# Delta rule: keys, queries, values and turned keys in two fixed sets of tiles, and four steps that load less

## The chip, the cores and the metric

The kernel runs on one core of a Trainium2 chip. The metric is the device time of one execution, in microseconds (us). Beside timed runs there is one profiled execution, with the time of every instruction and transfer.

## The reference, cut to what matters

The program is a two-layer backbone over 256 context tokens and 512 latent tokens of width 1024. Layer 0 mixes with a bidirectional gated delta rule, layer 1 with attention. The change touches only the delta rule of layer 0, which for one direction and one chunk of 64 tokens does this with its state `s`, a 128 x 128 matrix per head:

```python
def step(s, xs):
    qk_i, qd_i, kd_i, u_i, w_i, gl_i = xs
    v_new = u_i - jnp.einsum('bhcd,bhde->bhce', w_i, s)
    o = jnp.einsum('bhcd,bhde->bhce', qd_i, s) + jnp.einsum('bhcs,bhse->bhce', qk_i, v_new)
    s = s * gl_i[..., None, None] + jnp.einsum('bhcd,bhce->bhde', kd_i, v_new)
    return s, o

def bidir_delta(q, k, v, g, beta, s0_f, s0_b):
    o_f, s_f = chunk_gated_delta(q, k, v, g[:, 0], beta[:, 0], s0_f)
    ...
    o_b, s_b = chunk_gated_delta(fl(q), fl(k), fl(v), fl(g[:, 1]), fl(beta[:, 1]), s0_b)
    return o_f + fl(o_b), s_f, s_b
```

There are 16 value heads and 8 key heads. First the 4 context chunks are run from a zero state, both ways, then the 8 latent chunks from the two states that this leaves.

## The kernel before, in words

**Pairs of chunks.** The two directions run at the same time. A step takes one chunk of the forward direction and one of the backward direction, 64 + 64 = 128 partitions. Chunk p and chunk n - 1 - p make up pair t; there are 2 pairs of context and 4 of latent tokens. Each pair is met twice (`visit` 0 and 1), the second time with the directions exchanged, so there are 12 steps `s` = 0 to 11, which work on the pairs 0, 1, 1, 0, then 2, 3, 4, 5, 5, 4, 3, 2.

**What a step needs from DRAM.** The keys k (`k_d`), the queries q (`q_d`), the values v (`v_d`, as two halves of 64 partitions), the turned keys kt (`kt_d`), all four the same at both visits of a pair; and the inverse T (`t_d`) and the decayed product Q K (`qk_d`), which differ by visit. Each of k, q, each half of v, T, Q K and kt is a transfer of 512 KB. Each step but step 0 loads all of it. Step 0 needs no k and q, because its state is zero; its T, Q K, kt and v are loaded ahead by `first_matrices` and `first_values` (L1026 to L1034).

**Where it lies.** Odd steps take tiles of the pool `ch`, made at L1526. Even steps take tiles of the pool `even`: four buffers of the tag `df` (`even_tile`, L1018) for T, Q K, kt and k, and the tag `C` (`values_tile`, L1015) for v. The queries take two buffers of the tag `kq1` in turn. The pool `ch` stands where the pool of the stage before stood, so its first loads can begin only when that stage has let go of the memory.

**The work of a step.** A step is four parts of four heads (`x` = 4 s + p). `products(x)` (L1567) multiplies the state by k and by q (L1585; one matrix product group with k, one with q, for each of two key heads), subtracts from v on VectorE (L1588), scales the query product on ScalarE (L1591) and decays the state on GpSimd (L1594). `solve(x)` (L1600) applies T (L1611). `update(x)` (L1629) applies Q K (L1640) and kt (L1648). They are written in the order products(x), solve(x-1), update(x-2).

**What sets the order.** On TensorE, VectorE, ScalarE and GpSimd the order is as written (`manual_schedule`, L1771). The SyncE queue (SP), which issues the loads, is not held to it: a planner places its loads as soon as their tile is free by its reckoning, among loads that are free at once in the order of the program. Each engine and queue then runs strictly in the order so found. The load helpers are

```python
    def matrices_loaded(t, visit, Tt, QK, kt):
        dma(Tt, t_d[t, :, visit])
        dma(QK, qk_d[t, :, visit])
        return dma(kt, kt_d[t]).ins
```

and `values_loaded` (L1009), which issues the two halves of v. `mark` holds a step's last load; the first loads of the next stage's weights and gates (L1812) are queued behind it at steps 7, 8, 9 and 10.

Of the kernel before, what the change touches and what calls it, by code (L numbers as in the profile page):

```python
# [8 lines left out]
F32 = mybir.dt.float32  # L9
# [8 lines left out]
P = 128  # L18
# [5 lines left out]
QH, VH = 8, 16  # L24
# [45 lines left out]
def pair_info(t):  # L70
    if t < 2:
        return t, 4, 0
    return t - 2, 8, NCTX
# [13 lines left out]
def backbone(tc, a, out):  # L87
    nc = tc.nc
    V, S, G, T = nc.vector, nc.scalar, nc.gpsimd, nc.tensor
    dma = nc.sync.dma_start  # L90
# [8 lines left out]
    def dtile(shape, name):  # L99
        return dram.tile(shape, F32, tag=name, name=name)  # L100
# [6 lines left out]
    k_d = dtile([NT, P, QH, P], "k_d")  # L107
    q_d = dtile([NT, P, QH, P], "q_d")
    kt_d = dtile([NT, P, QH, P], "kt_d")
# [4 lines left out]
    t_d = dtile([NT, P, 2, VH, 64], "t_d")  # L114
    qk_d = dtile([NT, P, 2, VH, 64], "qk_d")
# [70 lines left out]
    def rsqrt_steps(x, mul, out=None, room=None):  # L186

        n = x.shape[1]
        rcount[0] += 1
        y, t = (rsp.tile([P, NT * VH], F32, tag=f"rs{i}", name=f"rs{i}_{rcount[0]}")[:, 0:n] for i in range(2))  # L190
        if room is not None:
            t = room
        yi = y.bitcast(I32)
        steps = [
            lambda: V.tensor_scalar(x, x, mul, EPS, ALU.mult, ALU.add),
            lambda: V.tensor_scalar(yi, x.bitcast(I32), -0.5, float(0x5F3759DF), ALU.mult, ALU.add),
        ]
        for i in range(3):
            to = (x if out is None else out) if i == 2 else y
            steps += [  # L200
                lambda: V.scalar_tensor_tensor(t, x, -0.5, y, ALU.mult, ALU.mult),
                lambda: V.tensor_tensor(t, t, y, ALU.mult),
                lambda to=to: V.scalar_tensor_tensor(to, t, 1.5, y, ALU.add, ALU.mult),
            ]
        return steps
# [797 lines left out]
# [6 lines that stand above are left out]
    def values_loaded(t, v, h0=0, h1=VH):  # L1009
        p, n, base = pair_info(t)  # L1010
        for hf, c in ((0, p), (1, n - 1 - p)):
            c += base // 64
            dma(v[hf * 64:hf * 64 + 64, h0:h1], v_d[c // 2, c % 2 * 64:c % 2 * 64 + 64, h0:h1])

    def values_tile(s):  # L1015
        return room["even"].tile([P, 2, 32, 32], F32, tag="C", name=f"cv_{s}").rearrange("p a b c -> p (a b c)").rearrange("p (h d) -> p h d", d=P)

    def even_tile(s, nm):  # L1018
        return room["even"].tile([P, VH, 64], F32, tag="df", name=f"c{nm}_{s}", bufs=4)

    def by_key_heads(x):
        return x.rearrange("p h c -> p (h c)").rearrange("p (h d) -> p h d", d=P)

    opening = {}

    def first_matrices():  # L1026
        T_, QK, kt = (even_tile(0, nm) for nm in ("T", "QK", "kt"))
        opening["m"] = T_, QK, by_key_heads(kt)
        matrices_loaded(0, 0, *opening["m"])
# [112 lines left out]
    last = {}  # L1142
    T0 = 134

    def kept(name, piece):
        last[name] = piece
        return piece
# [29 lines left out]
    ck = Piece("DVE", 0.4, 0.0, biases_kept, after=[pv], holds=[("tr", pv)], lands=0.1, slack=0.1)  # L1177
# [17 lines left out]
    for q in range(4):  # L1195
# [7 lines left out]
        for k in (2 * q, 2 * q + 1):  # L1203
            y_ = None
            for i in range(2):
                f = at + 2.5 * (k % 2) + 0.6 * i
# [43 lines left out]
    for h in range(QH):  # L1250
# [4 lines left out]
        else:  # L1255
            wh, wl = k_weights(h, t0)
            g, owners = [], []
            for i in range(2):
                n = 1 if h == 1 else 4
# [28 lines left out]
    c = []  # L1288
# [48 lines left out]
    for n, (c, h) in enumerate(heads):  # L1337
        t0 = T0 + n * SLOT
        w = kept(("w", n), Piece("SP", 0.4, t0 - 30, w_load, n, takes=["w"], sent=1.3, since=-99.0))
# [38 lines left out]
    def keys_and_rows(t, queries, due, since=0.0, after=()):  # L1378
        k = Piece("SP", 1.0 + queries, due, keys_loaded, t, queries, takes=["kq", "kq"], sent=1.3 + 1.3 * queries, since=since, after=list(after) + row_loads[-2:-1], behind=late_pieces)
        for v in range(2):  # L1380
            row_loads.append(Piece("SP", 2.0 - queries, due, decay_rows, t, v, not queries, takes=["df"], sent=2.4, since=since, after=row_loads[-1:] or [k]))
        return k, row_loads[-2:]
# [18 lines left out]
    for t, due in enumerate(T0 + x for x in (-14, -15, 45, 126, 140, 160)):  # L1401
        k, r = keys_and_rows(t, False, due - 12, since=max(T0 + 24.0, due - 14))
# [39 lines left out]
    for t, due in enumerate(T0 + x for x in (275, 280, 320, 685, 710, 820)):  # L1442
        k, r = keys_and_rows(t, True, due - 12, after=[last["stored", "q", h] for h in range(QH)])
# [4 lines left out]
        for v in range(2):  # L1448
            G_ = (t, v) not in ((0, 0), (0, 1), (1, 0), (1, 1), (2, 0), (2, 1), (3, 0), (3, 1), (4, 0), (4, 1), (5, 0), (5, 1))
            pr = Piece("POOL" if G_ else "DVE", 2.42 if G_ else 1.22, due + 8, q_prod, t, v, G if G_ else V, port=1, after=[ma, d_[v]], holds=[("df", r[v]), (f"KQ{v}", ma)], lands=0.1)  # L1450
            qprev.append(pr)
            kept(("QK", t, v), Piece("SP", 1.3, due + 14, q_store, t, v, after=[pr], holds=[("df", r[v])], sent=2.2))
    Piece("DVE", 2.4, T0 + N * SLOT - 5, lambda: [f_() for f_ in rsqrt_steps(rq.rearrange("p t h -> p (t h)"), 1.0)], after=[last["rq", h] for h in range(QH)], since=T0 + 376.0)

    at = T0 + N * SLOT - 60
    Piece("SP", 1.2, at, first_matrices, after=[last["T", 0], last["QK", 0, 0], last["QK", 5, 0], last["QK", 5, 1]], takes=["df", "df", "df"], sent=5.0)
    fv = []
# [12 lines left out]
    ch = ch_c.__enter__()  # L1470
# [52 lines left out]
    if True:  # L1523
        ch.tile([P, 4, P], F32, tag="r0", name="r_0", bufs=1)
        St = [ch.tile([P, 2, 2, P], F32, tag=f"S{hh}", name=f"S{hh}", bufs=1) for hh in range(QH)]
        for tag, shape, n in (("vn", [P, 4, P], 2), ("vd", [P, 4, P], 2), ("T", [P, VH, 64], 1), ("v", [P, VH, P], 1), ("QK", [P, VH, 64], 1),  # L1526
                              ("kt", [P, QH, P], 1), ("kq0", [P, QH, P], 1), ("kq1", [P, QH, P], 2), ("o", [P, 4, P], 2), ("r1", [P, 4, P], 1)):
            for i in range(n):
                ch.tile(shape, F32, tag=tag, name=f"{tag}_first{i}", bufs=n)

        def where(s):
            n, sl, base = (4, s, 0) if s < 4 else (8, s - 4, 2)
            visit = 0 if sl < n // 2 else 1
            return base + (sl if visit == 0 else n - 1 - sl), visit

        loads = {}
        mark = [None]

        def load_step(s):
            nm = f"_{s}"  # L1540
            t, visit = where(s)
            if s == 0:
                (Tt, QK, kt), v = opening["m"], opening["v"]
                loads[s] = (None, kt, v, Tt, QK)
                return
            if s % 2:
                Tt = ch.tile([P, VH, 64], F32, tag="T", name="cT" + nm, bufs=1)
                v = ch.tile([P, VH, P], F32, tag="v", name="cv" + nm, bufs=1)
                QK = ch.tile([P, VH, 64], F32, tag="QK", name="cQK" + nm, bufs=1)
                kt = ch.tile([P, QH, P], F32, tag="kt", name="ckt" + nm, bufs=1)  # L1550
            k0 = ch.tile([P, QH, P], F32, tag="kq0", name="ck" + nm, bufs=1) if s % 2 else by_key_heads(even_tile(s, "k"))
            if not s % 2:
                Tt, QK = even_tile(s, "T"), even_tile(s, "QK")
                kt, v = by_key_heads(even_tile(s, "kt")), values_tile(s)
            kq = [k0, ch.tile([P, QH, P], F32, tag="kq1", name="cq" + nm)]
            for w, src in enumerate((k_d, q_d)):
                dma(kq[w], src[t])
            values_loaded(t, v)
            mark[0] = matrices_loaded(t, visit, Tt, QK, kt)
            loads[s] = (kq, kt, v, Tt, QK)  # L1560

        live = {}
        prq = [pcx.tile([P, 2, 4, P], F32, tag=tag, name=f"{tag}_all", bufs=1) for tag in ("pr", "pq")]
# [1 line left out]
        def products(x):  # L1567

            s, p = divmod(x, 4)
            if p == 0:  # L1570
                load_step(s)
# [362 lines left out]
    for n in range(32):  # L1934
# [5 lines left out]
        if n in (16, 19, 21, 24):  # L1940
            k0 = {16: 0, 19: 2, 21: 4, 24: 6}[n]
# [35 lines left out]
        if n in (18, 20, 23, 25):  # L1977
            k0 = {18: 0, 20: 2, 23: 4, 25: 6}[n]
# [217 lines left out]
    def q_cosines(p, t):  # L2196
        x = q_bank(p, t).rearrange("p (h d) -> p h d", h=2)
        o = tmp.tile([P, 2, P], F32, tag="qr", name=f"qr{p}{t}", bufs=2)
        V.tensor_tensor(o, x, bcast(cg[0][:, t], 1, 2), ALU.mult)
        return o  # L2200
# [179 lines left out]
    for u in range(32 + 4):  # L2380
        piece = pieces1[u] if u < len(pieces1) else None
        last = (q_products, 0, 3) if u == 0 else pieces1[u - 1] if u <= len(pieces1) else None
# [6 lines left out]
        o = None  # L2389
        if last and last[0] is q_products:  # L2390
            q_squares(*last[1:])
            o = q_cosines(*last[1:])
# [20 lines left out]
        for half in range(2):  # L2413
            if piece and piece[0] is q_products:
                q_products(*piece[1:], range(half * 4, half * 4 + 4))
            elif piece:
                k0 = 4 * (u % 2) + 2 * half
# [29 lines left out]
        if u == 23:  # L2447
# [4 lines left out]
            for k in range(KT):  # L2452
                w = wp.tile([P, D], F32, tag="w", name=f"wf{k}", bufs=3)
# [149 lines left out]
```

## Time and profile before

| | |
|---|---|
| median of 3 runs | 1144.64 us (1141.11 to 1145.9) |
| time of the profiled execution | 1139.69 us |
| its span | 1137.5 us |
| TensorE busy (matmul) | 1106.4 us, 97% |
| VectorE, ScalarE, GpSimd busy | 787.5, 746.9, 603.1 us |
| bytes moved | 208.69 MB |
| the twelve steps | from about 535.4 to 712 us of the span |

PE is TensorE's matmul, PEld its weight load, DVE is VectorE, ACT is ScalarE, POOL is GpSimd, SPq and ACTq are the queues from which SyncE and ScalarE issue transfers. In a timeline a row has the start, the duration, the engine, the line, the operation, output <- inputs, the number of instructions and in brackets the idle time before it with what ended it. In a table of transfers the last number is the time from issue to landing. Names lose their numbers: `cq` is the queries of any step, `ck` the keys, `cv` the values, `cT`, `cQK` and `ckt` the three matrices. `q1` is the transfer queue of SP, `q10` that of ACT, `q8` fetches TensorE's instructions.

### The profile page before, as it was taken

What the parts mean: (1) busy time and instruction counts of PE and PEld (TensorE: products, weight loads), DVE (VectorE), ACT (ScalarE), POOL (GpSimd) and SP (SyncE); (2) the same over time, 40 slices, a digit from 0 to 9 for tenths busy, and PEclk for the clock granted to TensorE, in tenths of its full rate; (3) what the DMA queues carried; (4) which work ended last, traced back from release to release, by engine and by line L of the source; (5) the groups of instructions that cost most, each with busy time, mean ns of one, the idle gap of its engine ahead of it and who ended that gap; (6) DMA issues with size and microseconds to landing.
All of it is one profiled execution on the core that took longest, in us unless ns stands there. A gap on an engine that the chain in (4) does not pass through costs nothing. (4 is left out here: it accounts for less than half of the span.)

```text
span 1137.5 us, 27228 instructions
## 1 busy us (share of the span) xinstructions
PE 1106.4 (97%) x10511; PEld 903.7 (79%) x10511; DVE 787.5 (69%) x1628; ACT 746.9 (66%) x1990; POOL 603.1 (53%) x525
## 2 busy tenths in 40 slices
PE   5999999999999999999999999999999999999997
PEld 2677788888888888888666666788877889989886
DVE  4785666688889988774678788445555477667647
ACT  4453554477787888756689888875776356666731
POOL 0564111329999999960675598656744353130820
PEclk9999999999999999999999999999999999999999
DMA  9489753765738887665998994676854112101323
GB/s 366 180 305 324 253 159 118 228 174 171 219 129 245 280 233 222 182 229 164 280 279 249 276 257 116 207 213 183 247 148 139 37 58 73 38 19 57 111 75 93
DMA packets 117106, 208.69 MB, mean 183 GB/s; under 512 B 12113, under 2 KB 76786, under 8 KB 111730
## 3 DMA queue, kind: packets, MB, share of 16 engines
q1 hardware_dynamic: 97202, 195.71, 55.8%
q10 hardware_dynamic: 19776, 11.25, 3.3%
q8 instruction: 83, 1.36, 0.5%
q14 instruction: 45, 0.37, 0.1%
HBM read 166.16 MB, written 40.67 MB: 182 GB/s over the span
## 5 line engine op out<-in xcount | busy, mean ns | idle before, releaser
L1768 PE MATMUL po<-woh,y 128*128 128x512 f32 x384 | 129.3, 401 | 0.0
L1706 POOL TENSOR_TENSOR wol<-wo,woh 128x1024 fp32r<-128x1024 f32 x32 | 77.3, 2416 | 54.3 <-ACT woh L1699 51.1
L810 POOL TENSOR_TENSOR X<-X,tmp 128x62 f32<-128x62 f32 (+15 forms) x93 | 99.5, 1070 | 7.3
L1594 POOL TENSOR_TENSOR S<-S,glb 128x512 f32<-128x512 f32 x80 | 81.8, 1044 | 36.4 <-PE ks L1585 36.1
L809 POOL TENSOR_TENSOR tmp<-L,X 128x62 f32<-128x62 f32 (+15 forms) x93 | 91.0, 979 | 6.7
L929 PE MATMUL g_z<-uh,wh_z 128*128 128x512 f32 (+1 forms) x256 | 88.0, 344 | 0.0
L929 PE MATMUL g_v<-uh,wh_v 128*128 128x512 f32 (+1 forms) x256 | 87.9, 344 | 0.0
L944 DVE SCALAR_TENSOR_TENSOR acc_v<-g_v,cwv,acc_v 128x510 f32<-128x510 f32 (+3 forms) x128 | 77.7, 614 | 14.7 <-ACT acc_v L936 11.3
L929 PE MATMUL g_z<-ul,wh_z 128*128 128x512 f32 (+1 forms) x256 | 86.2, 337 | 0.5 <-issue 0.5
L929 PE MATMUL g_v<-ul,wh_v 128*128 128x512 f32 (+1 forms) x256 | 86.1, 336 | 0.0
L929 PE MATMUL g_v<-uh,wl_v 128*128 128x512 f32 (+1 forms) x256 | 86.1, 336 | 0.0
L929 PE MATMUL g_z<-uh,wl_z 128*128 128x512 f32 (+1 forms) x256 | 86.1, 336 | 0.0
L1768 PEld LDWEIGHTS po<-woh,y 128*128 128x128 f32 x384 | 72.3, 188 | 15.5 <-issue 0.3
L1768 PE MATMUL po<-wol,y 128*128 128x512 f32 x192 | 75.5, 393 | 0.0
L1734 DVE SCALAR_TENSOR_TENSOR pt<-pt,og,z 128x128 f32<-128x128 f32 x96 | 34.4, 358 | 33.3 <-PE pt L1725 31.0
L555 POOL TENSOR_TENSOR kt<-kt,kss 128x768 f32<-128x768 f32 x8 | 11.6, 1472 | 85.6 <-DVE kss L183 57.0
L1585 PE MATMUL ks<-S,ck 128*64 128x256 f32 x352 | 55.5, 392 | 0.9 <-ACT o L1591 0.9
L1662 DVE TENSOR_TENSOR S<-su,S 128x512 f32<-128x512 f32 x80 | 51.5, 686 | 5.1 <-PE su L1648 3.4
L1588 DVE SCALAR_TENSOR_TENSOR r<-ks,negV,cv 128x128 f32<-128x128 f32 x176 | 52.4, 344 | 3.6 <-DMA cv<-v_d 1.9
L1585 PE MATMUL ks<-S,cq 128*64 128x256 f32 x352 | 53.7, 379 | 0.0
L929 PEld LDWEIGHTS g_z<-ul,wh_z 128*128 128x128 f32 x256 | 48.6, 190 | 5.4 <-issue 0.7
L929 PEld LDWEIGHTS g_z<-uh,wh_z 128*128 128x128 f32 x256 | 48.5, 190 | 5.2
(469 smaller groups left out, 3341.5 us busy)
## 6 DMA issues: line engine op xcount, KB each, us to landing
aw<-in_ada_late SPq DMA_DIRECT2D x16, 1024.0 KB, 7.5
wo<-in_dn_w_out SPq DMA_DIRECT2D x32, 512.0 KB, 3.9
cv<-v_d SPq DMA_DIRECT2D x22, 512.0 KB, 9.6
aw<-in_ada_first SPq DMA_DIRECT2D x8, 1024.0 KB, 11.4
w_z<-in_dn_w_in SPq DMA_DIRECT2D x16, 512.0 KB, 6.2
w_v<-in_dn_w_in SPq DMA_DIRECT2D x16, 512.0 KB, 4.8
v_d<-vt ACTq DMA_DIRECT2D x16, 384.0 KB, 4.2
cT<-t_d SPq DMA_DIRECT2D x12, 512.0 KB, 9.1
```

The costliest lines, as they stand in the source:

```text
L555: G.tensor_tensor(kt, kt, bcast(r[:, h % 2 * NT:(h % 2 + 1) * NT], 2, P), ALU.mult)
L809: G.tensor_tensor(tv, bcast(L[:, :, j + 1:, j], 3, j + 1), bcast(X[:, :, j, 0:j + 1], 2, n), ALU.mult)
L810: G.tensor_tensor(X[:, :, j + 1:, 0:j + 1], X[:, :, j + 1:, 0:j + 1], tv, ALU.subtract)
L929: T.matmul(ps[:, :m], w[:, k], u[:, k, c0:c0 + m], start=k == 0 and n_ == 0, stop=k == KT - 1 and n_ == 2)
L944: V.scalar_tensor_tensor(acc[:, c0 + lo:c0 + hi], ps[:, lo + j - 2:hi + j - 2], cwv[:, j, ct:ct + 1], acc[:, c0 + lo:c0 + hi], ALU.mult, A ...
L1585: T.matmul(ks[r0:r0 + 64, w], kq[w][:, hh, r0:r0 + 64], St[hh][:, d], start=True, stop=True)
L1588: V.scalar_tensor_tensor(r[:, 2 * j + i], ks[:, 0, i], negV[:, visit, t, h:h + 1], v[:, h], ALU.mult, ALU.add)
L1594: G.tensor_tensor(St[hh], St[hh], bcast(g_, 3, P), ALU.mult)
L1662: V.tensor_tensor(St[hh], sj, St[hh], ALU.add)
L1706: G.tensor_tensor(wl, raws.pop(n), halves[n][0], ALU.subtract)
L1734: V.scalar_tensor_tensor(pj, pj, og, raw(z, off, [[st_, 2], [1, 64]]), ALU.mult, ALU.mult)
L1768: T.matmul(acc[nh], y[i][:, j, :], ww[k][:, nh * 512:(nh + 1) * 512], start=h == 0 and x == 0, stop=h == VH - 1 and x == 2)
```

## The change

The tiles for T, v, Q K, kt, k and q of the pool `ch` are made once, in the same sizes and the same order as before, and named: `qB` and `qA` stand where the two buffers of `kq1` stood. There are two sets of k, q, v, kt. Set A is the even pool's k, v and kt with `qA`; set B is the odd pool's k, v and kt with `qB`. Steps take the sets in the order A B B A B A B A A B A B. T and Q K go by even and odd step as before.

Steps 2, 8 and 9 work on the pair of the step before or of three steps before, whose set is still on the chip: they load only T and Q K. Step 3 finds v and kt of step 0 in set A and loads T, Q K, k and q. At step 1 the load of q is issued after T and Q K and ahead of kt; in the other steps that load it, it stays behind k. All else is as it was.

```diff
+        work = [(("vn", [P, 4, P], 2), ("vd", [P, 4, P], 2)), (("o", [P, 4, P], 2), ("r1", [P, 4, P], 1))]
+        odd = {}
...
+        for nm, shape in (("T", [P, VH, 64]), ("v", [P, VH, P]), ("QK", [P, VH, 64]), ("kt", [P, QH, P]), ("k", [P, QH, P]), ("qB", [P, QH, P]), ("qA", [P, QH, P])):
+            odd[nm] = ch.tile(shape, F32, tag=nm, name="c" + nm, bufs=1)
...
+        (T0, QK0, kt0), v0 = opening["m"], opening["v"]
+        homes = {"A": (by_key_heads(even_tile(0, "k")), odd["qA"], v0, kt0), "B": (odd["k"], odd["qB"], odd["v"], odd["kt"])}
+
         def load_step(s):
-            nm = f"_{s}"
             t, visit = where(s)
+            k, q, v, kt = homes["ABBABABAABAB"[s]]
+            Tt, QK = (odd["T"], odd["QK"]) if s % 2 else (T0, QK0)
+            loads[s] = ((k, q), kt, v, Tt, QK)
             if s == 0:
...
-            kq = [k0, ch.tile([P, QH, P], F32, tag="kq1", name="cq" + nm)]
-            for w, src in enumerate((k_d, q_d)):
-                dma(kq[w], src[t])
-            values_loaded(t, v)
-            mark[0] = matrices_loaded(t, visit, Tt, QK, kt)
-            loads[s] = (kq, kt, v, Tt, QK)
+            fresh = s not in (2, 8, 9)
+            if fresh:
+                dma(k, k_d[t])
+                if s > 1:
+                    dma(q, q_d[t])
+                if s != 3:
+                    values_loaded(t, v)
+            dma(Tt, t_d[t, :, visit])
+            last = dma(QK, qk_d[t, :, visit])
+            if s == 1:
+                dma(q, q_d[t])
+            if fresh and s != 3:
+                last = dma(kt, kt_d[t])
+            mark[0] = last.ins
```

More of the change, by code (lines that the diff above doesn't have):

```diff
@@ L1525, in backbone @@
         St = [ch.tile([P, 2, 2, P], F32, tag=f"S{hh}", name=f"S{hh}", bufs=1) for hh in range(QH)]
-        for tag, shape, n in (("vn", [P, 4, P], 2), ("vd", [P, 4, P], 2), ("T", [P, VH, 64], 1), ("v", [P, VH, P], 1), ("QK", [P, VH, 64], 1),
-                              ("kt", [P, QH, P], 1), ("kq0", [P, QH, P], 1), ("kq1", [P, QH, P], 2), ("o", [P, 4, P], 2), ("r1", [P, 4, P], 1)):
+        work = [(("vn", [P, 4, P], 2), ("vd", [P, 4, P], 2)), (("o", [P, 4, P], 2), ("r1", [P, 4, P], 1))]
+        odd = {}
+        for tag, shape, n in work[0]:
+            for i in range(n):
+                ch.tile(shape, F32, tag=tag, name=f"{tag}_first{i}", bufs=n)
+        for nm, shape in (("T", [P, VH, 64]), ("v", [P, VH, P]), ("QK", [P, VH, 64]), ("kt", [P, QH, P]), ("k", [P, QH, P]), ("qB", [P, QH, P]), ("qA", [P, QH, P])):
+            odd[nm] = ch.tile(shape, F32, tag=nm, name="c" + nm, bufs=1)
+        for tag, shape, n in work[1]:
             for i in range(n):
@@ L1537, in backbone @@
         mark = [None]
+        (T0, QK0, kt0), v0 = opening["m"], opening["v"]
+        homes = {"A": (by_key_heads(even_tile(0, "k")), odd["qA"], v0, kt0), "B": (odd["k"], odd["qB"], odd["v"], odd["kt"])}
         def load_step(s):
-            nm = f"_{s}"
             t, visit = where(s)
+            k, q, v, kt = homes["ABBABABAABAB"[s]]
+            Tt, QK = (odd["T"], odd["QK"]) if s % 2 else (T0, QK0)
+            loads[s] = ((k, q), kt, v, Tt, QK)
             if s == 0:
-                (Tt, QK, kt), v = opening["m"], opening["v"]
-                loads[s] = (None, kt, v, Tt, QK)
                 return
[L1546 to L1554, printed above, removed]
-            kq = [k0, ch.tile([P, QH, P], F32, tag="kq1", name="cq" + nm)]
-            for w, src in enumerate((k_d, q_d)):
-                dma(kq[w], src[t])
-            values_loaded(t, v)
-            mark[0] = matrices_loaded(t, visit, Tt, QK, kt)
-            loads[s] = (kq, kt, v, Tt, QK)
+            fresh = s not in (2, 8, 9)
[12 more added lines that the diff above has]
+            mark[0] = last.ins
         live = {}
```

## The prediction

> **What bounds the kernel now.** I read the page first, for the share of each engine.
>
> ```profile
> span 1137.5 us, 27228 instructions
> PE 1106.4 (97%) x10511; PEld 903.7 (79%) x10511; DVE 787.5 (69%) x1628; ACT 746.9 (66%) x1990; POOL 603.1 (53%) x525
> ```
>
> TensorE is busy nearly throughout, but that is an average. So I cut the delta rule's stretch into its steps, each from its first product to the next step's (stretch, then the busy time of PE, PEld, DVE, ACT, POOL, the granted clock, the DMA share and GB/s).
>
> ```profile
> 535.38:542.20 6.82, 4.93 (x114) 3.35 (x113) 4.01 (x13) 3.46 (x7) 1.19 (x2) 1.00 1.04 201
> 542.20:557.30 15.10, 15.10 (x260) 9.78 (x257) 10.97 (x26) 10.35 (x30) 9.33 (x10) 1.00 0.86 273
> 557.30:574.96 17.66, 15.59 (x261) 10.10 (x257) 12.15 (x29) 13.04 (x41) 13.17 (x12) 1.00 1.02 297
> 574.96:590.06 15.10, 15.10 (x258) 9.79 (x257) 12.39 (x29) 11.31 (x36) 12.39 (x12) 1.00 1.01 276
> 680.66:695.76 15.10, 15.10 (x260) 9.78 (x256) 12.43 (x29) 14.37 (x53) 14.10 (x17) 1.00 0.81 234
> ```
>
> A step takes 15.10 us, all of it PE, and it takes as long where the transfer engines are 81% busy as where they are 101% busy. So the loads cost nothing as such; they cost only where a product waits for one. Step 2 (557.30 to 574.96) alone is longer, by 17.66 - 15.10 = 2.56 us. That is the most that taking loads away can give in these steps. The timeline of PE and DVE shows where it sits:
>
> ```profile
> 560.10 1.04 PE L1648 MATMUL su<-vd,ckt 64*64 64x256 f32 x16
> 560.67 1.13 DVE L1588 SCALAR_TENSOR_TENSOR r<-ks,negV,cv 128x128 f32<-128x128 f32 x4 [1.85 <-DMA cv<-v_d]
> 562.06 0.65 PE L1585 MATMUL ks<-S,ck 128*64 128x256 f32 x4 [0.91 <-ACT o L1591]
> ...
> 569.61 0.65 PE L1585 MATMUL ks<-S,ck 128*64 128x256 f32 x4
> 571.97 0.60 PE L1640 MATMUL pq_all<-vn,cQK 64*64 64x128 f32 x13
> 573.73 0.32 PE L1640 MATMUL pq_all<-vn,cQK 64*64 64x128 f32 x2 [1.16 <-issue]
> 574.96 0.65 PE L1585 MATMUL ks<-S,ck 128*64 128x256 f32 x4
> ```
>
> A quarter of a step is 15.10 / 4 = 3.775 us. The second quarter of step 2 begins at 562.06 instead of 557.30 + 3.775 = 561.08: 0.98 us late, because DVE waited 1.85 us for v, then ACT for DVE, then PE for the buffer that ACT empties. The fourth quarter lasts 574.96 - 569.61 = 5.35 us, 1.58 us too long, with PE standing between two like matmuls for no reason that the profile shows ("issue"). The two make 2.56.
>
> **The opening, where one load moves.** Next I read the queue of SP at step 1, and the landing times of the transfers issued between 530 and 549 us.
>
> ```profile
> 490.52 0.98 SPq L1557 DMA_DIRECT2D ck<-k_d  x1
> 530.50 0.83 SPq L1557 DMA_DIRECT2D ck<-k_d  x1
> 531.38 0.42 SPq L1557 DMA_DIRECT2D cq<-q_d  x1
> 531.85 1.10 SPq L1013 DMA_DIRECT2D cv<-v_d  x2
> 533.04 0.53 SPq L1005 DMA_DIRECT2D cT<-t_d  x1
> 533.61 0.45 SPq L1006 DMA_DIRECT2D cQK<-qk_d  x1
> 536.25 0.34 ACTq L852 DMA_DIRECT2D t_d<-Tt  x1
> 548.35 0.32 SPq L1007 DMA_DIRECT2D ckt<-kt_d  x1
> 549.35 0.32 SPq L1557 DMA_DIRECT2D cq<-q_d  x1
> ```
>
> ```profile
> cv<-v_d SPq DMA_DIRECT2D x2, 512.0 KB, 8.4
> t_d<-Tt ACTq DMA_DIRECT2D x1, 1024.0 KB, 12.1
> ck<-k_d SPq DMA_DIRECT2D x1, 512.0 KB, 4.1
> cq<-q_d SPq DMA_DIRECT2D x1, 512.0 KB, 6.6
> cT<-t_d SPq DMA_DIRECT2D x1, 512.0 KB, 12.8
> cQK<-qk_d SPq DMA_DIRECT2D x1, 512.0 KB, 14.9
> ckt<-kt_d SPq DMA_DIRECT2D x1, 512.0 KB, 3.9
> ```
>
> Start plus landing time: k at 534.6, q at 538.0, v at about 540.3, T at 545.8, Q K at 548.5. The six loads, 3 MB, land in the order of issue, the last 18.0 us after the first issue, while a 1 MB store of ACT shares the same engines until 536.25 + 12.1 = 548.35. And this is when PE wants them:
>
> ```profile
> 542.20 0.65 PE L1585 MATMUL ks<-S,ck 128*64 128x256 f32 x4
> 542.68 0.60 PE L1585 MATMUL ks<-S,cq 128*64 128x256 f32 x4
> 547.85 0.67 PE L1611 MATMUL pr_all<-r,cT 64*64 64x128 f32 x16
> 552.11 0.62 PE L1640 MATMUL pr_all<-vn,cQK 64*64 64x128 f32 x16
> 552.55 1.04 PE L1648 MATMUL su<-vd,ckt 64*64 64x256 f32 x16
> ```
>
> q is wanted at 542.68, T at 547.85, Q K at 552.11, kt at 552.55. Today each is there: q with 4.7 us to spare, T with 2.0, Q K with 3.6, kt (548.35 + 3.9 = 552.25) with 0.3.
>
> **The change part by part.** *Loads removed.* Steps 2, 8 and 9 lose five each (k, q, two halves of v, kt), step 3 loses three: 18 transfers of 512 KB, 9 MB of the 208.69. At steps 3, 8 and 9 nothing waits for them, so this gives 0: PE's own 15.10 us are the cover. At step 2 the late v is no longer loaded, so the 0.98 us go. For the 1.58 us there are bounds: 0 if it has nothing to do with traffic, 1.58 if the fetch of PE's instructions stood behind the loads. Between 571 and 574 us the transfer engines show
>
> ```profile
> q1 hardware_dynamic: 234, 0.88, 95.0%
> q8 instruction: 1, 0.02, 2.9%
> ```
>
> and PE's own waits between 520 and 730 us hold this "issue" wait and no second one:
>
> ```profile
> PE pq_all L1640 <- issue: 1.2, 1, 1.2
> ```
>
> A fetch of instructions fell in just this stretch, among loads that took 95% of the engines. I take 1.58, since in the changed kernel steps 2 and 3 load 3 MB in place of 7. [...]
>
> *Fixed tiles.* Same sizes in the same order, so `qB` lies where step 1's q lay. Each load waits for the last reader of the same place, two steps back, as before: 0. The k that went out at 490.52 for step 2 was for the even pool's tile, which is now A's k and is filled for step 3: 0. If it is not sent early, see the second rival.
>
> *q of step 1 moved behind two halves of v, T and Q K.* On SP the four others move up by q's 0.47 us (531.85 - 531.38). Q K then goes out at 533.14 and takes its 0.45, so q goes out at about 533.6 in place of 531.38. The work of the engines is the same, 3 MB issued before ACT's store; only the order is new. By order of issue Q K takes T's place (545.8) and q takes Q K's place: 548.5. PE asks at 542.68. PE takes its work in order, so behind that product stand the second head pair, the last `solve` of step 0 and its last two updates; ACT, POOL and DVE wait for these, and so do T and Q K of step 2, whose tiles they free. Cost: 548.5 - 542.68 = 5.8 us. From below: a transfer that runs alone took 3.9 (kt), which would bring q at 537.5 and cost 0. From above: q could be held to the end of both of ACT's stores, after the second of which SP issued at 549.35: 6.7. I take 5.8, for q's neighbours in that queue took 12.8 and 14.9 us, not 3.9.
>
> [...]
>
> *What the delay covers.* Everything behind shifts by 5.8 us. kt of step 1 still goes out at 548.35 and now has 6.1 us to spare. T and Q K of step 2 shift with the products that free them and with those that use them, and have k, q, v and kt of step 2 no longer around them. q of step 3 lies where step 2's q lay and, with no last reader to wait for, can follow kt in that q's place. None becomes late. The weights and gates of the next stage, queued behind a step's last load, follow Q K in place of kt at steps 8 and 9; PE's full steps cover that too.
>
> *Sum.* +5.8 - 0.98 - 1.58 = +3.2 us. PE has no slack in the steps behind (15.10 of 15.10 in the rows above), so this reaches the end: 1139.69 + 3.2 = 1142.9 us on the profiled execution's scale. That execution lay 4.95 us under the median of the runs (1144.64), so for the median I say 1144.64 + 3.2 = 1147.9.
>
> **The rivals.** *First: q comes in time.* Either the planner sends q ahead of v after all, or the engines serve q beside its neighbours. Then only the gain is left: -2.56, 1142.1 us. For it: q needs to gain only 5.8 us, and alone a load takes 3.9. Against it: the landing times above rise strictly with the place in the queue, and the order in the trace was the order of the program.
>
> *Second: q waits for ACT's store.* The waits of SP's queue show that kt was held by something that isn't its data:
>
> ```profile
> SPq L1007 <- DMA t_d<-Tt: 14.3, 1, 14.3
> SPq L1557 <- DMA z_d<-sil_z: 0.6, 1, 0.6
> ```
>
> kt went out at 548.35, the moment ACT's t_d store landed, and the next load once ACT's z_d store had. From the first store to kt the program has two stores and six loads: it looks as if only eight transfers may be open, and the ninth waits for the first. In the changed order q is the eighth, with nothing to spare. If one more transfer is placed ahead of it (A's k, should it not go out at 490), q is the ninth: issued at 548.35, landed 3.9 later at 552.25, a wait of 9.6 us, and 9.6 - 2.56 = +7.0: 1151.6 us, slower. It decides from one transfer on. Against it: that k has its tile free at 490 as before.
>
> *Third: the change does not reach the time.* q is only a few us late, say landing with T's row at 545.8: +3.2 - 2.56 = +0.6, 1145.2 us.
>
> **How the numbers follow.** The forecast has 0.60, with a range of its own from 1145.5 to 1149.5 (the stall 4.9 to 6.7, the 1.58 gone or not, less or more a microsecond of measurement). First rival 0.18, second 0.12, third 0.10. The runs before spread from 1141.11 to 1145.9, so a difference under 0.5% (5.7 us) can't be told from no change here. A gain of 5.7 has no place in this profile, where the steps hold 2.56; 0.04 is for the measurement. Slower by over 0.5%, beyond 1150.4, is the second rival and an upper part of the forecast: 0.12 x 0.8 + 0.60 x 0.15 = 0.19. Within: 0.77. The range goes from the first rival less the spread, 1141, to the second, 1152.
>
> **What would show it.** In the changed profile: the first product with q at step 1 waits for `cq`, starting near 548.5 of a like span and about 6 us behind the product with k; step 2 lasts 15.1 with no wait for `cv` and no "issue" wait; the other steps stay at 15.10; about 199 MB are moved. Wrong if q lands before T, if q is issued at 548 or later, or if step 2 keeps its 17.66.

## The result and the profile after

Timed side by side, 22 runs each, the changed kernel takes 1145.09 us (median; 1142.24 to 1147.69) and the kernel before 1142.57 us (1139.08 to 1145.9). The ratio is 1.0023, with a 95% interval of 1.0014 to 1.0032, so the change costs 1.6 to 3.7 us, about 2.5. That is a loss and not a gain, and it is less than the 0.5% that the prediction set as the bound of "no change". The profiled execution takes 1142.61 us, against 1139.69 before.

The page of the changed kernel begins with the span and the engines' busy time; further down it has the bytes moved.

```profile
span 1140.6 us, 27187 instructions
...
PE 1106.7 (97%) x10511; PEld 904.0 (79%) x10511; DVE 788.7 (69%) x1628; ACT 748.6 (66%) x1990; POOL 603.3 (53%) x525
...
DMA packets 115026, 199.24 MB, mean 175 GB/s; under 512 B 11826, under 2 KB 76499, under 8 KB 110163
```

The 9 MB are gone (208.69 before), and TensorE's busy time is what it was (1106.4 before). So look at the steps. These are steps 1, 2, 3 and 8 of the changed kernel, in the same columns as before: stretch and length, busy time of PE, PEld, DVE, ACT and POOL, granted clock, DMA share, GB/s.

```profile
540.84:562.99 22.15, 17.11 (x258) 10.62 (x256) 11.06 (x26) 10.36 (x30) 9.41 (x10) 0.85 0.48 170
562.99:578.09 15.10, 15.10 (x260) 9.79 (x256) 12.29 (x29) 11.93 (x37) 12.36 (x12) 1.00 0.32 95
578.09:593.19 15.10, 15.10 (x260) 9.78 (x256) 12.43 (x29) 12.65 (x41) 13.30 (x13) 1.00 0.83 243
638.49:653.59 15.10, 15.10 (x260) 9.78 (x256) 12.28 (x29) 13.60 (x49) 8.61 (x10) 1.00 0.32 107
```

Step 2 has come down from 17.66 to 15.10 us. Step 1 has gone up from 15.10 to 22.15, that is by 7.05, and its row shows two things that were not there before: PE is busy for 17.11 us of it where 15.10 had done, and the granted clock is 0.85. The steps behind are 15.10, with the transfer engines at 83% as with the engines at 32%.

SP's queue in the opening shows where q of step 1 (`cqB`) now stands, behind two halves of v, T and Q K, and the view of landings says how long it took.

```profile
528.87 1.00 SPq L1557 DMA_DIRECT2D ck<-k_d  x1
529.93 1.09 SPq L1013 DMA_DIRECT2D cv<-v_d  x2
531.12 0.53 SPq L1562 DMA_DIRECT2D cT<-t_d  x1
531.70 0.45 SPq L1563 DMA_DIRECT2D cQK<-qk_d  x1
532.19 0.55 SPq L1565 DMA_DIRECT2D cqB<-q_d  x1
544.55 0.32 SPq L1567 DMA_DIRECT2D ckt<-kt_d  x1
```

```profile
cQK<-qk_d SPq DMA_DIRECT2D x1, 512.0 KB, 12.4
cqB<-q_d SPq DMA_DIRECT2D x1, 512.0 KB, 14.3
```

Issued at 532.19 and 14.3 us on its way, q is there at 546.5. PE's timeline shows who waited for it.

```profile
540.84 0.65 PE L1591 MATMUL ks<-S,ck 128*64 128x256 f32 x4
546.52 1.12 PE L1591 MATMUL ks<-S,cqB 128*64 128x256 f32 x4 [5.04 <-DMA cqB<-q_d]
547.43 1.07 PE L1591 MATMUL ks<-S,ck 128*64 128x256 f32 x4
548.29 1.07 PE L1591 MATMUL ks<-S,cqB 128*64 128x256 f32 x4
...
551.67 0.65 PE L1591 MATMUL ks<-S,ck 128*64 128x256 f32 x4
```

The first quarter of step 1 lasts 551.67 - 540.84 = 10.83 us in place of 3.775. PE stood for 5.04 us of the 7.05 that this is longer. The other 2.0 are in the groups behind the wait: a group of four matmuls that takes 0.60 to 0.65 us elsewhere takes 1.07 to 1.12 here. The stretches of one microsecond each say why; the last number but two of a row is the granted clock.

```profile
542.00:543.00 1.00, 0.00 (x0) 0.00 (x0) 0.24 (x1) 0.00 (x0) 0.00 (x0) 1.00 1.01 422
543.00:544.00 1.00, 0.00 (x0) 0.00 (x0) 0.00 (x0) 0.00 (x0) 0.00 (x0) 0.75 1.07 425
544.00:545.00 1.00, 0.00 (x0) 0.00 (x0) 0.00 (x0) 0.00 (x0) 0.00 (x0) 0.50 0.67 263
...
549.00:550.00 1.00, 1.00 (x18) 0.72 (x19) 0.60 (x2) 0.03 (x1) 0.55 (x1) 0.50 0.62 254
550.00:551.00 1.00, 1.00 (x32) 0.93 (x31) 0.01 (x1) 0.90 (x3) 0.49 (x1) 0.83 0.13 53
```

While PE stood, its clock fell to half (by the 0.75 about half way between 543 and 544), and it stayed there until about 550.3, some 3.8 us after the products had begun again.

One more step differs. Before, step 7 was longer than the others too:

```profile
635.36:651.02 15.66, 15.66 (x260) 10.17 (x256) 12.41 (x29) 13.63 (x49) 8.61 (x10) 1.00 0.94 273
```

In the changed kernel it lasts 15.10 us, like every step behind the first. So the two traces differ by +7.05 us in step 1, -2.56 in step 2 and -0.56 in step 7, +3.9 in all. The spans differ by 3.1, since other stages also differ from one execution to the next: step 0's first solve, from which the first row of steps before was counted, begins at 533.72 here and at 535.38 before.

### The profile page after: what moved, and what is told of

It is laid out like the page before. It is cut to its first block, busy times and chain, and to the rows that moved or that the text cites. A ratio compares the mean times of both kernels' runs of the same rounds, so it can differ in the third digit from the quotient of the medians.

```text
span 1140.6 us, 27187 instructions
## 1 busy us (share of the span) xinstructions
PE 1106.7 (97%) x10511; PEld 904.0 (79%) x10511; DVE 788.7 (69%) x1628; ACT 748.6 (66%) x1990; POOL 603.3 (53%) x525
## 3 DMA queue, kind: packets, MB, share of 16 engines
q8 instruction: 83, 1.36, 0.5%
## 5 line engine op out<-in xcount | busy, mean ns | idle before, releaser
L929 PEld LDWEIGHTS g_z<-uh,wl_z 128*128 128x128 f32 x256 | 48.5, 189 | 5.2
L929 PEld LDWEIGHTS g_v<-uh,wh_v 128*128 128x128 f32 x256 | 48.5, 190 | 5.1
```

The source lines that it names most:

```text
L929: T.matmul(ps[:, :m], w[:, k], u[:, k, c0:c0 + m], start=k == 0 and n_ == 0, stop=k == KT - 1 and n_ == 2)
```

## The experiments

The theory: the change is two edits with opposite signs, a late q (a wait, and then a slow clock) and 18 loads fewer. The rivals: the lost time comes from the changed tiles or from something else in the opening; and on the other side, the gain in step 2 comes from the later start of step 2 and not from the loads. The ratios to the kernel before, each with its interval, make a square:

| | q of step 1 second in its queue | q of step 1 behind Q K |
|---|---|---|
| all loads | 1 (the kernel before) | 1.0029 [1.0014, 1.0044] |
| 18 loads fewer | 0.9971 [0.9957, 0.9984], 0.9965 [0.9949, 0.9981], 0.9965 [0.9950, 0.9981] | 1.0023 [1.0014, 1.0032] |

### q of step 1 second again, the rest of the change kept

```diff
                 dma(k, k_d[t])
-                if s > 1:
-                    dma(q, q_d[t])
+                dma(q, q_d[t])
...
-            if s == 1:
-                dma(q, q_d[t])
```

> The changed kernel with one edit undone: at step 1 q is loaded right behind k again. If the place in the queue is the cause: q lands about 6.6 us after its issue, ahead of its product, the first quarter of step 1 lasts 3.8 us in place of 10.8, step 2 keeps its 15.10, and the time is 2.5 us under the kernel before (ratio about 0.998) and 5 to 7 us under the changed kernel. If the fixed tiles or the missing loads themselves cost the time: the wait at step 1 goes, but the ratio to the kernel before stays above 1.000.

The same kernel was run on three chips, the second and third time next to other experiments:

> The version with q second once more, beside the two kernels that it is compared with: ratio 0.9957 to 0.9984 as before. If that first measurement was a chance of the chip: nearer to 1.000.

> The kernel with q of step 1 second in its queue once more, on the chip and among the runs of the kernel with eight loads put back, so that the two can be set side by side: ratio 0.9965 to 0.997, no wait for q at step 1, every step 15.10 us. Whether TensorE shows issue waits in the opening is open: one profile of this kernel had 2.1 us of them and the other none.

Measured: 1138.48, 1137.61 and 1138.56 us, against 1142.32, 1142.16 and 1142.72 of the kernel before among the same runs. It is faster than both kernels, than the one before by 0.29% to 0.35% (1.8 to 5.8 us by the intervals). Steps 1 and 2 of the second of these profiles, and q's landing:

```profile
542.02:557.12 15.10, 15.10 (x260) 9.78 (x256) 10.97 (x26) 10.33 (x30) 9.32 (x10) 1.00 0.74 269
557.12:572.22 15.10, 15.10 (x260) 9.79 (x256) 12.29 (x29) 11.89 (x37) 12.37 (x12) 1.00 0.33 100
```

```profile
cqB<-q_d SPq DMA_DIRECT2D x1, 512.0 KB, 7.0
```

Four transfers fewer ahead of it halve q's way, from 14.3 to 7.0 us, and with that go the wait, the slow clock and all of the 7.05. The span is 1134.2 us, 6.4 less than with q behind Q K. So the loss is that one line. The fixed tiles are not to blame, for they are the same here.

The three profiles of this one kernel differ in another thing. The first has two pauses of PE for which the profile names no cause, among its waits in the opening:

```profile
PE su L1651 <- issue: 1.3, 1, 1.3
...
PE pw L861 <- issue: 0.8, 1, 0.8
```

The second has none, the third one of 0.5 us. This bears on the 1.58 us of the prediction. The page of the kernel before counts the transfers of instructions:

```profile
q8 instruction: 83, 1.36, 0.5%
q14 instruction: 45, 0.37, 0.1%
```

That `q8` serves TensorE is an estimate from the sizes: it moved 1.36 of these 1.73 MB (79%), and TensorE has 21,022 of the 27,228 instructions (77%). In that trace a transfer on `q8` ran from 571.15 to 572.52, among the loads that took 95% of the engines, and PE went on at 573.73, 1.2 us after its end. So the author takes such a pause for TensorE waiting for instructions whose transfer stood behind loads. That rests on times that lie close together; no run here shows what TensorE waited for.

### The kernel before, with only q of step 1 behind Q K

```diff
-            for w, src in enumerate((k_d, q_d)):
-                dma(kq[w], src[t])
+            dma(kq[0], k_d[t])
+            if s != 1:
+                dma(kq[1], q_d[t])
             values_loaded(t, v)
-            mark[0] = matrices_loaded(t, visit, Tt, QK, kt)
+            dma(Tt, t_d[t, :, visit])
+            dma(QK, qk_d[t, :, visit])
+            if s == 1:
+                dma(kq[1], q_d[t])
+            mark[0] = dma(kt, kt_d[t]).ins
```

> The kernel before with that one edit done: at step 1 q is loaded behind T and Q K, nothing else changes and all loads stay. If the place in the queue is the cause: the product with q waits about 5 us, then TensorE runs at half its clock for about 4 us more, step 1 lasts about 22 us, and the time is 5 to 7 us over the kernel before (ratio 1.005 to 1.006); less, if the later start of step 2 lets v land in time and so gives back 1 us. If the wait belongs to the fixed tiles: no wait, ratio 1.000.

Measured: 1145.6 us. PE's timeline at step 1, and the stretch of step 2:

```profile
541.17 0.65 PE L1590 MATMUL ks<-S,ck 128*64 128x256 f32 x4
545.67 1.12 PE L1590 MATMUL ks<-S,cq 128*64 128x256 f32 x4 [3.85 <-DMA cq<-q_d]
...
551.42 0.65 PE L1590 MATMUL ks<-S,ck 128*64 128x256 f32 x4
```

```profile
562.74:577.84 15.10, 15.10 (x260) 9.78 (x256) 12.28 (x29) 11.89 (x37) 12.38 (x12) 1.00 0.88 244
```

The quarter lasts 10.25 us, 6.48 too long: 3.85 of waiting and 2.6 of slow clock. And step 2 lasts 15.10 us although all its loads are there and the transfer engines are 88% busy. The late v and the pause of the kernel before have gone without a load removed: everything that PE does comes some 6 us later, the loads do not, and v is there in time. That is the rival on the gain's side, and it is right. The time is 3.3 us over the kernel before, not the 5 to 7 that were expected, since step 2 gives 2.56 back. With q late, the 18 loads fewer are worth nothing that these runs can tell (1.0023 against 1.0029). With q in time they are worth 0.29% to 0.35%.

### The wait filled with work

```diff
-                for w in range(2):
+                for w in (0, *[2] * (12 if x == 4 and j == 0 else 0), 1):
                     for d in range(2):
                         r0 = (visit ^ d) * 64
+                        if w == 2:
+                            T.matmul(ks[r0:r0 + 64, 1], kq[0][:, hh, r0:r0 + 64], St[hh][:, d], start=True, stop=True)
+                            continue
```

The changed kernel, with the product with k repeated twelve times ahead of the first product with q. Nothing is left out; the repeats are overwritten.

> The changed kernel, with TensorE kept at work while it waits: ahead of the first product with q at step 1, the product with k is repeated twelve times (24 product groups, about 5.2 us) into the place that the product with q then overwrites. No work is left out. If the idle time lets the clock fall: the granted clock stays at 1.00 through step 1, q is used at once or nearly so, the first quarter lasts about 8.9 us in place of 10.8, and the time is 2 us under the changed kernel (ratio to the kernel before about 1.001). If the slow products behind the wait come from something else (the transfers then under way): they stay at 0.91 us a group, the quarter stays at 10.8 or grows.

Measured: 1143.59 us, ratio 1.0011 [1.0000, 1.0023]. The timeline, and the stretch of the quarter:

```profile
543.23 5.35 PE L1592 MATMUL ks<-S,ck 128*64 128x256 f32 x48
548.40 0.60 PE L1594 MATMUL ks<-S,cqB 128*64 128x256 f32 x4
```

```profile
542.74:551.70 8.96, 8.96 (x116) 5.90 (x113) 2.51 (x6) 1.70 (x6) 2.05 (x2) 1.00 0.79 287
```

The product with q begins 548.40 - 542.74 = 5.66 us after the product with k, as in the changed kernel (5.68). But the clock stays at 1.00, the group behind takes 0.60 in place of 1.12, and the quarter is 8.96 us in place of 10.83. The 1.87 us between them are the clock alone: PE did more work and was done sooner. The ratios point the same way (1.0011 against 1.0023), though their intervals overlap.

### q one place earlier, and one place later

First, q between T and Q K:

```diff
             dma(Tt, t_d[t, :, visit])
-            last = dma(QK, qk_d[t, :, visit])
             if s == 1:
                 dma(q, q_d[t])
+            last = dma(QK, qk_d[t, :, visit])
```

> The changed kernel with q of step 1 one place further ahead: k, v, T, q, Q K, kt. If transfers land in the order of issue, q lands about 2 to 3 us earlier than behind Q K, near 11 us after its issue: the product with q waits about 2 us in place of 5, too short for the clock to fall, and the first quarter lasts about 6 us; ratio to the kernel before about 1.000. If place does not matter and q only competes with the store of ScalarE's queue: the wait stays at 5 us and the ratio at 1.002.

Measured: 1142.1 us, ratio 0.9993 [0.9978, 1.0007]: the change comes out even. From PE's timeline and the stretches of a microsecond:

```profile
543.38 1.12 PE L1654 MATMUL su<-vd,ckt 64*64 64x256 f32 x6 [1.23 <-issue]
...
546.61 1.12 PE L1591 MATMUL ks<-S,cqB 128*64 128x256 f32 x4 [1.05 <-DMA cqB<-q_d]
```

```profile
543.00:544.00 1.00, 0.62 (x6) 0.30 (x5) 0.00 (x0) 0.00 (x0) 0.00 (x0) 0.66 0.97 406
```

q landed 13.3 us after its issue at 533.27, only a microsecond sooner on its way than one place further back, but PE came to it later in this profile. The wait for q is 1.05 us. The clock had gone to half even before, in a pause of 1.23 us that followed one of 0.64, and the product with k just ahead was slow already. Counted from step 0's first solve (535.59 here, 533.72 in the changed kernel) q is there 1.8 us sooner, a little less than the 2 to 3 that were expected; by the times the place buys 0.3%, some 3.4 us. The quarter lasts 7.19 us and not 6, since the clock fell all the same, 0.60 on average over the quarter, though the wait was shorter than the 2 us that were expected to be too short for that. But short pauses do not always cost the clock. The first profile of the kernel with q second has the same pauses at the same products, with 0.64 us ahead of this one, and its products ran at their usual pace, 0.66 us for these six in place of 1.12, and 0.60 to 0.65 for the groups behind:

```profile
543.31 0.66 PE L1651 MATMUL su<-vd,ckt 64*64 64x256 f32 x6 [1.26 <-issue]
```

Then q behind kt, so that it is the ninth open transfer:

```diff
-            if s == 1:
-                dma(q, q_d[t])
             if fresh and s != 3:
                 last = dma(kt, kt_d[t])
+            if s == 1:
+                last = dma(q, q_d[t])
```

> The changed kernel with q of step 1 behind kt too: k, v, T, Q K, kt, q. If only eight transfers may be open: kt is now the eighth and goes out at once, near 532 us, and q is the ninth and goes out only as the t_d store of ScalarE's queue lands, near 544 to 546 us, then lands in under 5 us. The product with q waits 7 to 8 us, the time is 2 to 3 us over the changed kernel (ratio about 1.004 to 1.005). If kt waited for a reason of its own (its tile): kt still goes out near 544 us, and q behind it.

Measured: 1147.5 us, ratio 1.0036 [1.0015, 1.0056]. SP's queue, its waits, and PE's waits in the opening:

```profile
533.24 0.46 SPq L1565 DMA_DIRECT2D ckt<-kt_d  x1
547.69 0.32 SPq L1567 DMA_DIRECT2D cqB<-q_d  x1
```

```profile
SPq L1567 <- DMA t_d<-Tt: 14.0, 1, 14.0
```

```profile
PE pw L861 <- issue: 4.5, 1, 4.5
PE ks L1591 <- DMA cqB<-q_d: 3.4, 1, 3.4
```

The two loads have changed roles. kt, which waited for ACT's store in the kernel before (L1007, until 548.35) and in the changed one (L1567, until 544.55), goes out at once at 533.24, and q, whose tile is free, is held 14.0 us by a store that has nothing to do with its data. That is what the second rival said of the ninth transfer. The wait for q is only 3.4 us because PE itself came 4.5 us late to this step, by a pause in the stage before for which the profile names no cause.

### Is a load that nobody waits for free?

Three kernels put loads back into the one with q second, with the same values. The first reloads q, both halves of v and kt of pair 0 at step 2, and v and kt once more at step 3, where the changed kernel leaves them out:

```diff
+            if s == 2:
+                dma(homes["A"][1], q_d[0])
+                values_loaded(0, v0)
             if fresh:
                 dma(k, k_d[t])
                 dma(q, q_d[t])
-                if s != 3:
-                    values_loaded(t, v)
+                values_loaded(t, v)
             dma(Tt, t_d[t, :, visit])
             last = dma(QK, qk_d[t, :, visit])
-            if fresh and s != 3:
+            if s == 2:
+                dma(kt0, kt_d[0])
+            if fresh:
                 last = dma(kt, kt_d[t])
```

> The kernel with q of step 1 right behind k, with the removed traffic of steps 2 and 3 put back as loads that nobody waits for early: at step 2 also q of set A, the halves of v and kt of pair 0 are loaded into set A, and at step 3 v and kt once more (the same values as lie there already). v of step 2 is still taken from the tile on the chip. If the 1.58 us of the kernel before came from the fetch of TensorE's instructions behind the loads: an issue wait of 0.5 to 1.6 us is back in steps 1 to 3, without the wait for v, and the time is 0.5 to 1.6 us over the version with q second. If traffic has nothing to do with it: steps 2 and 3 stay at 15.10 and the two versions agree.

Measured: 1143.83 us, ratio 1.0021 [1.0007, 1.0034]. But one row of PE's waits takes the point away:

```profile
PE pr_all L1647 <- DMA cQK<-qk_d: 2.2, 1, 2.2
```

The loads put back stood ahead of step 2's Q K in SP's queue, and PE waited for it. Here are step 2, with this wait in it, and step 3:

```profile
559.49:577.12 17.63, 15.45 (x260) 10.06 (x256) 12.29 (x29) 11.90 (x37) 12.36 (x12) 1.00 0.85 219
577.12:592.98 15.86, 15.86 (x261) 10.32 (x257) 12.45 (x29) 12.96 (x43) 13.67 (x13) 1.00 1.01 295
```

So the time of this kernel is that of a late load and not of free ones. The clock stayed at 1.00 through a wait of 2.2 us. Step 3 is 0.76 us longer with no wait for data, in two places (a group of products with Q K takes 0.93 us at 583.26 and 0.88 at 591.20, in place of 0.62). That is in the range that was expected if the fetch stands behind loads, but this profile does not show that it was the fetch. The rest of the 6.2 us that this kernel takes more than the one with q second (1137.61) is not explained by its profile. The second, which reloads at steps 8 and 9 in the same manner, fell into the same trap:

> The version with q second, with the removed traffic of steps 8 and 9 put back: at each of the two the five loads are made again, into the set that the step doesn't use, with the values that lie there already. If loads that no product waits for cost nothing: steps 8 and 9 stay at 15.10 and the time agrees with the version with q second (within 0.6 us, the size of the one hitch that the kernel before shows near 648 us). If the lighter traffic itself speeds the kernel: 1 us or more slower.

Measured: 1150.56 us, ratio 1.0073 [1.0057, 1.0090]. One wait and the slow clock behind it make step 9 27.43 us long, 12.33 more than the others, of the 12.95 that this kernel takes more than the one with q second:

```profile
PE su L1658 <- DMA ckt<-kt_d: 10.0, 1, 10.0
```

```profile
663.92:691.35 27.43, 17.46 (x261) 10.70 (x257) 12.52 (x29) 14.35 (x53) 14.22 (x17) 0.81 0.88 243
```

The third puts eight loads (4 MB) behind a step's T and Q K, where no wanted load follows closely: v and kt of pair 0 at step 2, all five of pair 4 at step 8.

```diff
+            if s == 2:
+                values_loaded(0, v0)
+                last = dma(kt0, kt_d[0])
+            if s == 8:
+                dma(odd["k"], k_d[4])
+                dma(odd["qB"], q_d[4])
+                values_loaded(4, odd["v"])
+                last = dma(odd["kt"], kt_d[4])
             mark[0] = last.ins
```

> The kernel with q of step 1 second in its queue, and eight of the eighteen removed loads put back where nothing waits for them: at step 2 behind T and Q K the two halves of v and kt of pair 0, at step 8 behind T and Q K k, q, both halves of v and kt of pair 4; they write the same values once more, and 4 MB more are moved (about 203.5 MB in place of 199.2). Theory that a load costs only where a product waits for one: no wait for data in steps 2, 3, 8, 9 and 10, every step 15.10 us, and the ratio to the kernel before as without the loads, 0.9965 to 0.997. Rival, that traffic as such slows TensorE (by its instruction fetch or otherwise): steps 2, 3 and 8, 9 longer than 15.10 by a microsecond or more together with no data wait behind it, and a ratio of 0.998 or more.

Measured: 1138.46 us, ratio 0.9974 [0.9956, 0.9992], beside 1138.56 and 0.9965 of the kernel without them in the same runs. No product waits for data. But two steps, 2 and 7, in which the loads put back were under way (the last of them 12.9 and 7.3 us from issue to landing), are longer, and one of the two pauses has a row in PE's timeline:

```profile
556.66:572.39 15.73, 15.52 (x260) 9.85 (x257) 12.30 (x29) 11.90 (x37) 12.38 (x12) 1.00 0.70 198
...
632.79:648.96 16.17, 15.53 (x261) 10.05 (x257) 12.41 (x29) 13.62 (x49) 8.59 (x10) 1.00 0.88 240
```

```profile
645.83 0.43 PE L1596 MATMUL ks<-S,cqA 128*64 128x256 f32 x1 [0.64 <-issue]
```

By the times, eight loads cost nothing that can be told (the ratios differ by 0.0009, their intervals reach 0.0016 to 0.0018 to each side). By the profile, the two steps are 0.63 + 1.07 us longer where these loads were under way. The kernel without these loads has a longer step too, in the profile of the same runs, but for another reason:

```profile
541.19:557.36 16.17, 15.33 (x259) 9.86 (x256) 10.98 (x26) 10.24 (x30) 9.31 (x10) 1.00 0.78 269
```

```profile
548.20 0.32 SPq L1564 DMA_DIRECT2D ckt<-kt_d  x1
```

```profile
552.56 1.09 PE L1651 MATMUL su<-vd,ckt 64*64 64x256 f32 x16 [0.84 <-DVE O L1657]
```

kt of step 1, held behind ACT's store until 548.20, took 4.2 us to land, to 552.4, and the product with it begins at 552.56. The profile puts this wait down to the addition to O on VectorE, which ended at the same time, but that product neither reads nor overwrites what the addition uses. So kt, which had 0.3 us to spare before, is the next load to become late.

So the step times that were expected for both kernels were missed. The ratio of 0.9974 lies between what was expected without a cost of the loads (0.9965 to 0.997) and with one (0.998 or more). In this profile the two longer steps lie among loads that no product waits for, but no run shows that these loads made them longer; what eight of them cost on the whole is too small for these runs to tell.

## Why the prediction was right or wrong

**The forecast and what came.** +3.2 us was forecast and about +2.5 measured, 1.6 to 3.7 by the interval: right in sign and nearly in size. The level, 1147.9, was 2.8 us above the 1145.09 measured, which lies under the forecast's own range (1145.5 to 1149.5). The step that failed there is the last one, "for the median I say 1144.64 + 3.2 = 1147.9": the three runs of the kernel before gave 1144.64, and 22 gave 1142.57. On that base the same sum gives 1145.8. The range stands on the same base, and it does not follow from the terms that it names either: they give 1146.0 to 1151.4.

In the sum itself the step that failed is the size of the stall, 5.8 us: it put the slow clock behind the wait at nothing, and 7.05 were measured. The gain was also larger than the 2.56 that were read, 3.12 in the steps. So the near hit of the sum is in part luck: the traces differ by +3.9 us in the steps and the runs by +2.5. By the runs, q late costs 0.52% to 0.58% where the 18 loads are gone (5.9 to 6.6 us), and these loads gone give 0.29% to 0.35% where q is in time.

**"q of step 1 moved behind two halves of v, T and Q K ... I take 5.8".** The mechanism was right and the rows came as described. q went out behind Q K (532.19), took about as long as Q K had taken before (14.3 against 14.9 us), and the product with q began 5.68 us behind that with k ("about 6"). The wait itself was 5.04. The term was mis-sized at its end: it stopped at the landing. After 5 us without work the clock was half, and the work behind it cost 2.0 us more, 7.05 in all, which is above the upper bound of 6.7 that was named. The run with the wait filled shows that the 2.0 are the clock (1.87 by that comparison). In the profile of before nothing of the kind was to be seen, for its longest pauses of PE in these steps, 1.26 and 1.16 us, went by at a clock of 1.00.

The way back took 3.8 us here, from 546.5 to 550.3. In the kernel before with q late the products were slow from 545.67 until behind 550.19, and with kt late at step 9 from 676.87 until behind 680.54. On the way down the clock fell about 543.5 here, 2.0 us after the last product had ended at 541.49. But in the run with q behind T it fell about a pause of 1.23 us that followed one of 1.25 and one of 0.64, and through a wait of 2.18 us (Q K late at step 2) it stayed at 1.00. So these runs give no length of a pause from which on the clock falls.

**"At step 2 the late v is no longer loaded, so the 0.98 us go."** They went: step 2 has 15.10 us and PE no wait in it. But the reason given is not needed. With every load kept and q late they go as well, because v's deadline moves with PE while v does not. The prediction itself had PE's work later and asked only which loads that covers for the changed kernel; it did not ask what the delay alone does to the gain. The term stands in the sum either way, so the total did not suffer. What suffered is the account: once q was late, the 0.98 us did not need the loads to be taken away.

**"I take 1.58, since in the changed kernel steps 2 and 3 load 3 MB in place of 7."** It went: in the changed kernel step 2 holds no pause, with the transfer engines 32% busy in place of 102%. That the fetch of instructions was the cause was an estimate and is not shown: a transfer on `q8` ended 1.2 us before PE went on, among loads, and no run takes the two apart. And the loads taken away are not the only cure. With all loads kept and q late step 2 has no pause either, with the engines 88% busy.

**"Step 2 (557.30 to 574.96) alone is longer."** Not so: step 7 lasted 15.66 us, so the steps held 3.12 us and not 2.56. That 0.56 sits among loads too, those for step 8, with the transfer engines 94% busy over the step (three products that begin at 647.16 take 0.95 us), and "at steps 3, 8 and 9 ... this gives 0" missed it. It is gone in the changed kernel and in the second and third profile with q second, whose step 7 has 15.10 us; in the kernel with eight loads put back a pause is there again, 1.07 us at the same products.

**"Fixed tiles ... 0".** Borne out: the fixed tiles run at 1137.61 to 1138.56 us when q is second. The k for step 3 went out early, as had been said of it. Steps 3, 8 and 9 themselves were 15.10 us before and are 15.10 us now.

**The rivals.** The first, q in time, gave 1142.1, that is -2.56. It did not happen here, but it is the kernel with q second: 3.8 to 4.6 us faster by the medians, with the -2.56 inside its intervals. The second, nine open transfers, did not happen either, because q was the eighth; with one load more ahead it does, and q then goes out when ACT's store has landed, as it said. Its price of +7.0 was not reached in that run (1.0036, about 4 us), where PE came 4.5 us late to the step by a pause without a named cause. The third, q a few us late, is the kernel with q behind T: +0.6 was its price, and the ratio 0.9993 [0.9978, 1.0007] holds it.

## What to carry to other kernels

A load that is moved back in a shared queue costs its wait and then, behind the waits of 3.45, 3.85, 5.04 and 9.97 us in these runs, slow products (behind the 2.18 us none): price the work after the wait at the granted clock too, here 0.50 for 3.8 us, which cost 2.0 us more. Put loads in the order in which the products ask for them: here one line moved back turned a change worth -0.3% into one of +0.2%. When a delay is forecast, price every later stall again under that delay before crediting its disappearance to another part of the change. And take the base of a forecast from enough runs: three of this kernel lay 2 us too high.

## What was not expected of the hardware

The halved clock: 0.50 from about 543.5 to 550.3, with matmul groups at 1.07 us in place of 0.60, for a wait of 5 us. Pauses of 1.25, 0.64 and 1.23 us close together halved it in one run (0.50 from 544 to 550), and behind pauses of the same sizes at the same products in another the groups took their usual 0.60 us. What decides between the two no run here shows.

The pauses without a named cause, up to 4.5 us in one profile. In the kernel before, the one in step 2 ended 1.2 us after a transfer of instructions had; that TensorE waited for instructions there is the author's estimate. They differ between profiles of one kernel (2.1 us, none and 0.5 us in the opening of the three with q second), so a single profile of this kernel cannot place a microsecond or two.
